# A DiT block kernel: two gates' modulation computed in later FFNs, and no background dot beside a slice's last column tile

## The chip, the cores and the metric

The kernel runs on one core of one Trainium2 chip. A core has five engines that matter here: TensorE (PE in the profile; its weight loads are listed apart as PEld), VectorE (DVE), ScalarE (ACT), GpSimd (POOL) and SyncE (SP), whose queue issues nearly all DMA transfers. Each engine works through its own instructions in order; they wait for each other through semaphores. The metric is the device time of one execution in microseconds.

## The reference

Two layers of a diffusion transformer with width 1024, on 512 latent and 256 context tokens. Each layer is an FFN, a token mixer (a gated DeltaNet group beside a multi-head latent attention group), and a second FFN:

```python
m = silu(c) @ w_ada[l] + b_ada[l]            # 9 vectors of 1024 for the latent tokens, and 9 for the context
def pre_mod(x, g, m, slot):
    return rmsnorm(x, g) * (1 + m[3 * slot + 1]) + m[3 * slot]
def post_residual(x, y, g, m, slot, weight):
    return x + weight * m[3 * slot + 2] * rmsnorm(y, g)
def ffn_sublayer(x, m, slot, ...):            # d_ff = 2816
    h = pre_mod(x, g_pre, m, slot)
    y = (silu(h @ wg) * (h @ wu)) @ wd
    return post_residual(x, y, g_post, m, slot, 0.5)
for l in range(2):
    x = ffn_sublayer(x, m, 0, ...)            # first FFN
    x = post_residual(x, mixer(pre_mod(x, g, m, 1)), g, m, 1, 1.0)
    x = ffn_sublayer(x, m, 2, ...)            # second FFN; in layer 1 for the latent tokens alone
```

The nine vectors of a layer are numbered (slot, part): slot 0 is the first FFN, 1 the mixer, 2 the second FFN; part 0 is the shift, 1 the scale, 2 the gate that `post_residual` multiplies with. The modulation of a gate is therefore needed only when its sublayer's output is there.

## The kernel before

Everything is fp32. A weight or an activation is split into a rounded part `whi` or `gh` (type fp32r) and the rest `wlo` or `gl`, and each product is made of three matmuls: high by high, high by low, low by high. A weight tile comes by DMA into one of four buffers (`wraw`, 128x1024, 512 KB), ScalarE copies it to `whi` (L93) and GpSimd or VectorE subtracts to get `wlo` (L94).

**An FFN** (`ffn`, L522) takes the 22 column tiles of 128 of its hidden width in six slices of 4, 4, 4, 4, 2, 4 tiles. The first three tiles of slice 0 are computed as written in the reference. From the fourth on a tile is a *split tile* (`fast`, L586): gate and up products are formed from seven half products, 384 of the 768 tokens each (256 in the last FFN), with sums of weights and of activations formed on VectorE. The names in it: `prod` issues the 12 matmuls of a half product (L606 to L608); `u2`, `u4`, `c12`, `p1` are sums on VectorE; `out` (L611) forms the gated result at its end: an add (L614), a multiplication (L615), ScalarE's copy to `gh` (L616) and VectorE's subtraction to `gl` (L617). After a slice, `down` (L755) multiplies its tiles with the down weights and adds into y (eight row tiles, in pairs; L773, L774 and L776 are the matmuls with `gh`, `gl`, and `wlo`). Within the first pair the slice's last tile comes last.

**Background dots.** Of the modulation `m`, what is not needed at once is computed on VectorE beside the FFNs. `ada_bg(l, slot, parts, vecs)` (L351) puts one job for each of eight weight rows of each part on a list, and a closing one that adds the bias and forms the gate or scale; a job's DMA brings a row block of 512 KB (`abraw`, in the same four buffers as `wraw`), and its one or two dots (L241, 128x1024 with `srow`; one for the latent vector, one for the context vector; in the trace their output is named `adot` or `abraw`) reduce it to a column of `raw`. A *dot* below is one such L241 instruction of 128x1024; the short L241 rows of 128x1 read the sum out.

**What sets the order.** `pump` (L114) is called 58 times in an FFN: twice for tile 2, twice in each split tile, once for each row chunk in `down`, but never in the last slice's `down`. Each call adds `rate` to a credit, the number of jobs at the FFN's start divided by 57, and takes jobs from the list while the credit is at least 1. The credit is never set back: what is left goes on to the next FFN. Jobs that are left at the last slice's end are run by `flush` ahead of the residual (`p0` and `p2` in `body`, L1925 and L1957). The Tile framework's scheduler then orders each engine's instructions with a simulated timeline, within what the data and buffers allow; `high_priority` around the adds of a tile pulls these ahead of other work. So a dot stands not exactly where `pump` put it.

`body` (L1903) runs, for l = 0 and 1: `ada_bg` for the mixer and the second FFN, the first FFN, the mixer, for l = 0 `ada_bg` for layer 1's first FFN, and the second FFN. That gives 112, 48, 64 and 0 dots in the four FFNs.

Of the kernel before, what the change touches and what calls it, by code (L numbers as in the profile page):

```python
# [34 lines left out]
class K:  # L35
# [61 lines left out]
    def hp(self, on):  # L97
        return self.tc.high_priority(offset=on if on > 1 else None) if on else contextlib.nullcontext()
# [12 lines left out]
            self.ahead = nxt()  # L111
        fn(w)

    def pump(self):  # L114
        self.credit += self.rate
        if self.ahead is None and self.bg and self.bg[0][0]:
            self.ahead = self.bg[0][0]()
            return
        ran = False
        while self.credit >= 1 and self.bg:  # L120
            if self.bg[0][0] is None and ran:
                break
            ran = True
            self.credit -= 1
            self.bg_next()
# [396 lines left out]
    def ffn(self, l, i, slot, groups, post, begin=None):  # L522
# [7 lines left out]
        def loads(f, eng=None):  # L530
            return [self.load_w(d["wu"][l, i, f, u], eng=eng) for u in range(2)]
# [7 lines left out]
        def evac(j, pg, pu, off, n):  # L539
            for o in range(0, n, 256):  # L540
                sg = self.sg()[:, :256]
                c = slice(o, o + 256)
                with self.tc.high_priority():
                    nc.scalar.activation(sg, pg[:, c], AF.Silu)
                    nc.vector.tensor_tensor(out=sg, in0=pu[:, c], in1=sg, op=ALU.mult)  # L545
                gated(j, sg, off + o, 256)
# [32 lines left out]
        def combine_t1(F):  # L579

            for k in range(4):
                h, lo = F["t1"][k]
                nc.scalar.copy(h, self.y[k][:, :nh])
                nc.vector.tensor_sub(lo, self.y[k][:, :nh], h.bitcast(F32))

        def fast(f, j, F):  # L586


            lo_, hi_ = slice(0, 512), slice(512, 1024)
            wg, wu = self.raw(d["wu"][l, i, f, 0]), self.raw(d["wu"][l, i, f, 1])  # L590
            V = nc.vector
            w0 = self.cut(wg)
            w2 = self.cut(wu[:, hi_], 512, V)
            V.tensor_sub(wg[:, lo_], wg[:, lo_], wu[:, lo_])
            V.tensor_add(wu[:, lo_], wu[:, lo_], wu[:, hi_])
            V.tensor_sub(wu[:, hi_], wu[:, hi_], wg[:, lo_])
            V.tensor_sub(wg[:, hi_], wg[:, hi_], wu[:, hi_])
            w3 = self.cut(wu, eng=V)
            w1 = self.cut(wg, eng=V)

            def prod(w, half, xs):
                ps = self.bank()[:, :nh]
                for k in range(4):
                    c = slice(half * 512 + k * P, half * 512 + (k + 1) * P)
                    xh, xl = F[xs][k]
                    nc.tensor.matmul(ps, w[0][:, c], xh, start=k == 0, stop=False)  # L606
                    nc.tensor.matmul(ps, w[0][:, c], xl, start=False, stop=False)  # L607
                    nc.tensor.matmul(ps, w[1][:, c], xh, start=False, stop=k == 3)  # L608
                return ps

            def out(ps, u, sl, off):  # L611

                gx, gy = gh[j][:, off : off + nh], gl[j][:, off : off + nh]
                V.tensor_add(ps, u, ps)  # L614
                V.tensor_mul(ps, ps, sl)  # L615
                nc.scalar.copy(gx, ps)  # L616
                V.tensor_sub(gy, ps, gx.bitcast(F32))  # L617

            T = lambda n: self.sg(n)[:, :nh]
            hp = self.tc.high_priority  # L620
            ps = prod(w0, 0, "b11")
            p1 = T("p1")
            with hp():
                nc.scalar.copy(p1, ps)
            ps = prod(w3, 1, "t2")
            u2 = T("u2")
            with hp():
                V.tensor_add(u2, p1, ps)
            ps = prod(w0, 1, "b21")
            with hp():  # L630
                V.tensor_add(p1, p1, ps)
                nc.scalar.activation(p1, p1, AF.Silu)
            ps = prod(w3, 0, "t1")
            u4 = T("u4")
            with hp():
                V.tensor_add(u4, u2, ps)
            self.pump()
            ps = prod(w1, 1, "b22")
            c12 = T("c12")
            with hp():  # L640
                V.tensor_add(c12, u4, ps)
                nc.scalar.activation(c12, c12, AF.Silu)
            ps = prod(w1, 0, "t3")
            with hp():
                V.tensor_add(u2, u2, ps)
                out(ps, u4, c12, nh)
            ps = prod(w2, 0, "t4")
            with hp():
                out(ps, u2, p1, 0)
            self.pump()  # L650

        if begin is not None:
            next(begin)
        for s, nf in enumerate(SLICES):
            gh = [self.fp.tile([P, NT], F32R, tag=f"gh{j}", name=f"gh{j}") for j in range(nf)]
            gl = [self.fp.tile([P, NT], F32R, tag=f"gl{j}", name=f"gl{j}") for j in range(nf)]
            f0 = SL0[s]
# [68 lines left out]
            if s == 0:  # L726
                self.drain()
                F = combine()
            for j in range(j0, nf):
                if f0 + j > 2:  # L730
                    if f0 + j == 3:
                        combine_t1(F)
                    fast(f0 + j, j, F)
                    continue
                ps = []
                pre = s == 0 and j == 2 and W2
                W = [None, self.load_w(d["wu"][l, i, 2, 1])] if pre else loads(f0 + j)
                for u in range(2):
                    if pre and u == 0:
                        ps.append([(pl, 0, NL)] + ([(pc[:, :256], NL, NC)] if has_c else []))  # L740
                        self.pump()
                        continue
                    wh, wl = W[u]
                    outs = [(self.bank()[:, :n], off, n) for off, n in full]
                    for k in range(KT):
                        self.mm3(outs, wh[:, k * P : (k + 1) * P], wl[:, k * P : (k + 1) * P], k, k == 0, k == KT - 1)
                    ps.append(outs)
                    if u == 0:
                        self.pump()
                for (pg, off, n), (pu, _, _) in zip(*ps):  # L750
                    evac(j, pg, pu, off, n)
                self.pump()
# [1150 lines left out]
def body(tc, dram, out, stop=None):  # L1903
    k = K(tc, dram, out)
    nc = k.nc
    k.psp = k.pool("psum", space=PSUM)
    k.drp = k.pool("dram", space=DRAM)
    k.ph = 'start'
    k.consts()
    k.open_w()  # L1910
    k.open_z()
    k.open_f()
    k.ada_bg(0, 0, [2], [0, 1])
    for l in range(2):
        last = l == 1
        if l == 0:
            k.ada_bg(0, 1, [0, 1, 2], [0, 1])
            k.ada_bg(0, 2, [0, 1, 2], [0, 1])
        else:
            k.ada_bg(1, 1, [0, 1], [0, 1])  # L1920
            k.ada_bg(1, 1, [2], [0])
            k.ada_bg(1, 2, [0, 1, 2], [0])
        k.rate = len(k.bg) / 57

        def p0(g, ss):  # L1925
            k.flush()
            return k.post(l, 0, g, ss, nxt=(l, 1))

        k.ph = f'F1_{l}'
        k.ffn(l, 0, 0, GROUPS, p0, k.begin() if l == 0 else None)  # L1930
        k.mix_pre(l)
        k.drain()
        xd = k.dram_tile(f"xd{l}", [KT, P, NT])
        for kt in range(KT):
            nc.sync.dma_start(xd[kt], k.X[kt])
        k.close(k.fp)
        k.ph = f'M1_{l}'
        k.mix_in(l, last)
        k.close_z()
        k.close(k.wp)  # L1940
        k.ph = f'G_{l}'
        k.gdn(l, last)
        k.open_zs(range(6))
        k.gdn_out(l, last)
        k.ph = f'A_{l}'
        k.mla(l, last)
        if stop == f"o_{l}":
            for j in range(8):
                nc.gpsimd.dma_start(out[:, j, 0], k.zh[j].bitcast(F32))
                nc.gpsimd.dma_start(out[:, j, 1], k.zl[j].bitcast(F32))  # L1950
            return finish(k, False)
        k.open_f()

        def p1(g, ss):
            return k.post(l, 1, g, ss, nxt=(l, 2))

        def p2(g, ss):  # L1957
            k.flush()
            return k.post(l, 2, g, ss, final=last, nxt=(l + 1, 0))

        k.ph = f'O_{l}'
        k.mix_out(l, last, xd, p1)
        if not last:
            k.ada_bg(1, 0, [0, 1, 2], [0, 1])
        k.rate = len(k.bg) / 57
        k.ph = f'F2_{l}'
        k.ffn(l, 1, 2, GROUPS[1:] if last else GROUPS, p2)
        if last or stop:
            k.drain()
        if stop == f"f2_{l}":  # L1970
            return dump_x(k)
    finish(k)


def dump_x(k):
    for kt in range(KT):
        k.nc.sync.dma_start(k.out[:, kt], k.X[kt])
    finish(k)
# [31 lines left out]
```

## Time and profile before

| | |
|---|---|
| runs of the kernel | 3344.32, 3345.82, 3350.79 us (median 3345.82) |
| the profiled execution | 3344.23 us |
| its span in the trace | 3342.5 us |
| granted clock of TensorE, mean of the span | 0.951 |
| TensorE busy, matmuls | 3078.1 us (92%) |
| TensorE busy, weight loads | 2805.2 us (84%) |
| VectorE busy | 2545.8 us (76%) |
| ScalarE busy | 1376.5 us (41%) |
| GpSimd busy | 1359.4 us (41%) |

Busy time counts how long an engine had an instruction in work; matmuls are pipelined and their ends are modelled. The granted clock is a share of full speed, 2.4 GHz. TensorE is busy for 92% of the span, so what can be gained lies in its waits and in the stretches in which it runs at less than full clock. The share is a mean over stages with different limits, and the mixers' waits are in it as well.

### The profile page before, as it was taken

The page shows a single profiled execution, that of the slowest core. Times are in us where ns is not written, and L with a number is a line of the kernel's source. Part 1 is how long each engine was busy: PE and PEld are TensorE (multiplying, and loading weights), DVE is VectorE, ACT ScalarE, POOL GpSimd, SP SyncE. Part 2 cuts the span into 40 slices and gives each one's busy share as a digit, 9 for nine tenths or more (in the row PEclk, how much of TensorE's full clock was granted, in tenths as well). Part 3 has the DMA queues.
Part 4 walks back from the last instruction along what each step waited for, and adds up shares of the span by engine and source line. Part 5 has one row for each costly group of instructions (what it writes and reads, how often), then busy time and mean ns, then how long its engine had stood idle before and what let it go on. Part 6 is the DMA issues. An engine that isn't in the chain of part 4 may idle for free. (4 is left out here: it accounts for less than half of the span.)

```text
span 3342.5 us, 53690 instructions
## 1 busy us (share of the span) xinstructions
PE 3078.1 (92%) x20836; PEld 2805.2 (84%) x20836; DVE 2545.8 (76%) x4336; ACT 1376.5 (41%) x2600; POOL 1359.4 (41%) x1060
## 2 busy tenths in 40 slices
PE   7899999889898999999999799999988788899998
PEld 4799888877786788899999799999977676789998
DVE  7888888777779858677777977677687879876676
ACT  4332223454345645333324432323454445554343
POOL 5321221543556665322214522221554556753233
PEclk8999999989998999999999899999989899899999
DMA  6233343321310032223324233342322310223233
GB/s 232 89 127 119 114 144 103 120 68 50 111 47 27 21 107 83 89 95 107 101 70 145 68 122 120 120 145 89 108 91 58 102 46 5 88 77 114 89 108 95
DMA packets 149815, 318.68 MB, mean 95 GB/s; under 512 B 38184, under 2 KB 79528, under 8 KB 149560
## 3 DMA queue, kind: packets, MB, share of 16 engines
q1 hardware_dynamic: 149560, 315.25, 29.0%
q8 instruction: 163, 2.67, 0.3%
q14 instruction: 92, 0.75, 0.1%
HBM read 285.17 MB, written 30.03 MB: 94 GB/s over the span
## 5 line engine op out<-in xcount | busy, mean ns | idle before, releaser
L94 POOL TENSOR_TENSOR wlo<-wraw,whi 128x1024 fp32r<-128x1024 f32 (+1 forms) x228 | 589.5, 2595 | 1356.5 <-ACT whi L93 1261.1
L93 ACT CAST whi<-wraw 128x1024 fp32r<-128x1024 f32 (+2 forms) x482 | 469.0, 977 | 700.4 <-PE ps L774 341.6
L517 PE MATMUL ps<-zh,whi 128*128 128x256 f32 (+1 forms) x1208 | 394.1, 336 | 24.6 <-DVE sg L545 13.3
L606 PE MATMUL ps<-zh,whi 128*128 128x384 f32 (+1 forms) x1216 | 391.3, 322 | 3.5 <-DVE sg L545 2.9
L607 PE MATMUL ps<-zl,whi 128*128 128x384 f32 (+1 forms) x1216 | 390.8, 321 | 0.0
L608 PE MATMUL ps<-zh,wlo 128*128 128x384 f32 (+1 forms) x1216 | 390.3, 321 | 0.0
L518 PE MATMUL ps<-zl,whi 128*128 128x256 f32 (+1 forms) x1208 | 381.4, 327 | 4.1 <-DVE zl L475 4.1
L773 PE MATMUL ps<-gh,whi 128*128 128x512 f32 (+1 forms) x1008 | 349.4, 354 | 29.9 <-ACT gh L616 27.2
L520 PE MATMUL ps<-zh,wlo 128*128 128x256 f32 (+1 forms) x1208 | 352.5, 326 | 0.0
L774 PE MATMUL ps<-gl,whi 128*128 128x512 f32 (+1 forms) x1008 | 339.7, 352 | 12.1 <-DVE gl L617 12.1
L94 DVE TENSOR_TENSOR wlo<-wraw,whi 128x1024 fp32r<-128x1024 f32 (+1 forms) x254 | 289.2, 1139 | 41.2 <-ACT whi L93 39.7
L776 PE MATMUL ps<-gh,wlo 128*128 128x512 f32 (+1 forms) x1008 | 297.0, 351 | 0.0
L517 PEld LDWEIGHTS ps<-zh,whi 128*128 128x128 f32 x1208 | 240.0, 203 | 57.3 <-DVE sg L545 14.6
L518 PEld LDWEIGHTS ps<-zl,whi 128*128 128x128 f32 x1208 | 240.1, 199 | 23.7 <-DVE zl L475 5.1
L773 PEld LDWEIGHTS ps<-gh,whi 128*128 128x128 f32 x1008 | 192.3, 193 | 74.5 <-ACT gh L616 30.2
L606 PEld LDWEIGHTS ps<-zh,whi 128*128 128x128 f32 x1216 | 229.2, 189 | 5.6 <-DVE sg L545 1.9
L241 DVE CUSTOM_DVE_ANT_0 abraw<-abraw,srow 128x1024 f32<-128x1024 f32 x128 | 202.6, 1582 | 38.7 <-DMA abraw<-in_wat 36.4
L607 PEld LDWEIGHTS ps<-zl,whi 128*128 128x128 f32 x1216 | 229.2, 188 | 0.4
L608 PEld LDWEIGHTS ps<-zh,wlo 128*128 128x128 f32 x1216 | 229.0, 188 | 0.0
L774 PEld LDWEIGHTS ps<-gl,whi 128*128 128x128 f32 x1008 | 193.4, 192 | 42.0 <-DVE gl L617 16.5
L520 PEld LDWEIGHTS ps<-zh,wlo 128*128 128x128 f32 x1208 | 223.4, 199 | 6.1 <-POOL zl L475 0.6
L606 PE MATMUL ps<-t42h,whi 128*128 128x384 f32 (+1 forms) x608 | 197.8, 325 | 2.8 <-ACT whi L93 2.8
(394 smaller groups left out, 7686.4 us busy)
## 6 DMA issues: line engine op xcount, KB each, us to landing
wraw<-in_wu SPq DMA_DIRECT2D x176, 512.0 KB, 3.4
abraw<-in_wat SPq DMA_DIRECT2D x128, 512.0 KB, 4.1
wraw<-in_wd SPq DMA_DIRECT2D x88, 512.0 KB, 3.4
wraw<-in_wi SPq DMA_DIRECT2D x44, 512.0 KB, 3.3
wraw<-in_wo SPq DMA_DIRECT2D x16, 512.0 KB, 3.9
xs<-x SPq DMA_DIRECT2D x64, 128.0 KB, 1.7
x<-xs SPq DMA_DIRECT2D x64, 128.0 KB, 3.4
x<-in_x SPq DMA_DIRECT2D x48, 128.0 KB, 3.6
```

Of the source, the lines that this page charges most:

```text
L93: nc.scalar.copy(hi[:, :n], raw[:, :n])
L94: (eng or nc.gpsimd).tensor_sub(lo[:, :n], raw[:, :n], hi[:, :n].bitcast(F32))
L241: self.nc.vector.tensor_tensor_reduce(out=dst, in0=w, in1=self.srow[:, v, a:b], scale=1.0, scalar=start, op0=ALU.mult, op1=ALU.add, accum_ ...
L517: nc.tensor.matmul(ps, wh, self.zh[k][:, off : off + n], start=first, stop=False)
L518: nc.tensor.matmul(ps, wh, self.zl[k][:, off : off + n], start=False, stop=False)
L520: nc.tensor.matmul(ps, wl, self.zh[k][:, off : off + n], start=False, stop=last)
L606: nc.tensor.matmul(ps, w[0][:, c], xh, start=k == 0, stop=False)
L607: nc.tensor.matmul(ps, w[0][:, c], xl, start=False, stop=False)
L608: nc.tensor.matmul(ps, w[1][:, c], xh, start=False, stop=k == 3)
L773: nc.tensor.matmul(ps, wh[:, o : o + P], gh[j][:, off : off + n], start=j == 0, stop=False)
L774: nc.tensor.matmul(ps, wh[:, o : o + P], gl[j][:, off : off + n], start=False, stop=False)
L776: nc.tensor.matmul(ps, wl[:, o : o + P], gh[j][:, off : off + n], start=False, stop=j == nf - 1)
```

## The change

Two edits are made. First, `pump` takes an argument; a split tile that is the last of its slice calls it with a false value, and then it adds to the credit and starts no job, so that the jobs come at the next call, which is one in `down`. Second, the gates are put on the list later: the gate of layer 0's second FFN on the list of that FFN, layer 1's first gate on the list of the FFN that it belongs to, and layer 1's last gate on the list of the last FFN. The four FFNs get 96, 48, 72 and 8 dots. Lines from L116 on stand two further down than before.

```diff
-    def pump(self):
+    def pump(self, now=True):
         self.credit += self.rate
+        if not now:
+            return
...
-        def fast(f, j, F):
+        def fast(f, j, F, bg):
...
-            self.pump()
+            self.pump(bg)
             ps = prod(w1, 1, "b22")
...
-            self.pump()
+            self.pump(bg)
...
-                    fast(f0 + j, j, F)
+                    fast(f0 + j, j, F, j < nf - 1)
...
         if l == 0:
             k.ada_bg(0, 1, [0, 1, 2], [0, 1])
-            k.ada_bg(0, 2, [0, 1, 2], [0, 1])
+            k.ada_bg(0, 2, [0, 1], [0, 1])
         else:
+            k.ada_bg(1, 0, [2], [0, 1])
             k.ada_bg(1, 1, [0, 1], [0, 1])
             k.ada_bg(1, 1, [2], [0])
-            k.ada_bg(1, 2, [0, 1, 2], [0])
+            k.ada_bg(1, 2, [0, 1], [0])
...
-        if not last:
-            k.ada_bg(1, 0, [0, 1, 2], [0, 1])
+        if last:
+            k.ada_bg(1, 2, [2], [0])
+        else:
+            k.ada_bg(0, 2, [2], [0, 1])
+            k.ada_bg(1, 0, [0, 1], [0, 1])
```

VectorE, first FFN of layer 0, the last tile of slice 1, from the add to `c12` to the last `gl`, before (the rows left out read a dot's sum):

```order
L641 TENSOR_TENSOR c_1926<-u_1906,ps 128x384
L241 ISA adot,raw_1_0_140<-abraw,srow 128x1024
...
L645 TENSOR_TENSOR u_1876<-u_1876,ps 128x384
L614 TENSOR_TENSOR ps<-u_1906,ps 128x384
L241 ISA abraw,raw_1_0_140<-abraw,srow 128x1024
...
L614 TENSOR_TENSOR ps<-u_1876,ps 128x384
L241 ISA adot,raw_1_0_140<-abraw,srow 128x1024
...
L615 TENSOR_TENSOR ps<-ps,c_1926 128x384
L615 TENSOR_TENSOR ps<-ps,p_1861 128x384
L241 ISA abraw,raw_1_0_140<-abraw,srow 128x1024
...
L617 TENSOR_TENSOR gl_1390<-ps,gh_1386 128x384 x2
```

The same place in the changed kernel:

```order
L643 TENSOR_TENSOR c_1911<-u_1896,ps 128x384
L243 ISA adot,raw_1_0_140<-abraw,srow 128x1024
...
L223 TENSOR_TENSOR m_1_0_3511<-raw_1_0_140,cols 128x16
L647 TENSOR_TENSOR u_1866<-u_1866,ps 128x384
L616 TENSOR_TENSOR ps<-u_1896,ps 128x384
L243 ISA abraw,raw_1_0_140<-abraw,srow 128x1024
...
L616 TENSOR_TENSOR ps<-u_1866,ps 128x384
L617 TENSOR_TENSOR ps<-ps,c_1911 128x384
L617 TENSOR_TENSOR ps<-ps,p_1851 128x384
L619 TENSOR_TENSOR gl_1385<-ps,gh_1381 128x384 x2
L243 ISA adot,raw_1_0_140<-abraw,srow 128x1024
```

Between the add to `c12` and the last `gl` there were four dots and now are two; the dot between the last multiplication and `gl` has gone, and one that stood between the two adds of L614 (now L616) and the multiplications now follows `gl`.

VectorE in layer 1, the end of the output projection and the start of the last FFN: squares' sums (`be`, L403), copies to y (L1789) and the row factors' scaling (`rba`, L156), before:

```order
L403 TENSOR_TENSOR be<-be,bt 128x256
L432 SCALAR_TENSOR_TENSOR x_27757<-bt,m_1_2_20072,x_27757 128x256
L1789 COPY y_27718<-ps 128x256
L403 TENSOR_TENSOR be<-be,bt 128x256
L1789 COPY y_27719<-ps 128x256
L403 TENSOR_TENSOR be<-be,bt 128x256
L1789 COPY y_27720<-ps 128x256
L156 TENSOR_SCALAR rba<-rb 128x2
L403 TENSOR_TENSOR be<-be,bt 128x256
L156 TENSOR_SCALAR rba<-rb 128x2
```

The same place in the changed kernel:

```order
L243 ISA abraw,raw_2_2_28310<-abraw,srow 128x1024
...
L405 TENSOR_TENSOR be<-be,bt 128x256
L434 SCALAR_TENSOR_TENSOR x_27732<-bt,m_1_2_20600,x_27732 128x256
L1791 COPY y_27693<-ps 128x256
L405 TENSOR_TENSOR be<-be,bt 128x256
L243 ISA abraw,raw_2_2_28310<-abraw,srow 128x1024
...
L1791 COPY y_27694<-ps 128x256
L243 ISA abraw,raw_2_2_28310<-abraw,srow 128x1024
...
L405 TENSOR_TENSOR be<-be,bt 128x256
L1791 COPY y_27695<-ps 128x256
L243 ISA abraw,raw_2_2_28310<-abraw,srow 128x1024
...
L158 TENSOR_SCALAR rba<-rb 128x2
```

Four dots of the last FFN's list now stand among these rows, where none stood.

VectorE in layer 0's second FFN, from the weight sums of its first split tile (L595 to L597) to its first add (L628), before:

```order
L595 TENSOR_TENSOR wraw<-wraw 128x512
L545 TENSOR_TENSOR sg<-ps,sg 128x256 x3
L596 TENSOR_TENSOR wraw<-wraw 128x512
L537 TENSOR_TENSOR gl_12439<-sg,gh_12435 128x256 x3
L597 TENSOR_TENSOR wraw<-wraw 128x512
L94 TENSOR_TENSOR wlo<-wraw,whi 128x1024 x2
L628 TENSOR_TENSOR u_13148<-p_13133,ps 128x384
```

The same place in the changed kernel:

```order
L597 TENSOR_TENSOR wraw<-wraw 128x512
L547 TENSOR_TENSOR sg<-ps,sg 128x256 x3
L598 TENSOR_TENSOR wraw<-wraw 128x512
L243 ISA adot,raw_2_2_12389<-abraw,srow 128x1024
...
L539 TENSOR_TENSOR gl_12397<-sg,gh_12393 128x256 x3
L599 TENSOR_TENSOR wraw<-wraw 128x512
L243 ISA abraw,raw_2_2_12389<-abraw,srow 128x1024
...
L94 TENSOR_TENSOR wlo<-wraw,whi 128x1024 x2
L630 TENSOR_TENSOR u_13111<-p_13096,ps 128x384
```

Two dots now stand between the weight sums and the `wlo` subtractions of the summed weights. TensorE in layer 1's first FFN, in its first split tile behind the product with `b11` (`t42h` and `t42l`, `zh` and `zl`, `t` are the operands of the half products; four of the seven take the summed weights, whose `wlo` is cut last), before:

```order
L606 MATMUL ps<-t42h,whi 128x384
L607 MATMUL ps<-t42l,whi 128x384
L606 MATMUL ps<-zh_9567,whi 128x384
L607 MATMUL ps<-zl_9568,whi 128x384
L608 MATMUL ps<-zh_9567,wlo 128x384
L606 MATMUL ps<-zh_9569,whi 128x384
L607 MATMUL ps<-zl_9570,whi 128x384
L608 MATMUL ps<-t42h,wlo 128x384
```

The same place in the changed kernel, where the product with `zh_9567` is complete already:

```order
L608 MATMUL ps<-t42h,whi 128x384
L609 MATMUL ps<-t42l,whi 128x384
L608 MATMUL ps<-zh_9522,whi 128x384
L609 MATMUL ps<-zl_9523,whi 128x384
L608 MATMUL ps<-zh_9524,whi 128x384
L609 MATMUL ps<-zl_9525,whi 128x384
L608 MATMUL ps<-t_18077,whi 128x384
L609 MATMUL ps<-t_18077,whi 128x384
L608 MATMUL ps<-t42h,whi 128x384
L609 MATMUL ps<-t42l,whi 128x384
L610 MATMUL ps<-t42h,wlo 128x384
...
L610 MATMUL ps<-t42h,wlo 128x384 x2
```

Before, the `wlo` of a summed weight was wanted by the 20th matmul of the tile; now four products are begun without their `wlo`, one that takes no summed weight is run to its end, and the 45th matmul is the first that wants such a `wlo`. In layer 0's second FFN it is the 45th before and now.

## Rows read from the trace of the kernel before

**Rows 1.** Windows of three FFNs' bodies: stretch, us, busy (count) by engine, clock, DMA, GB/s.

```profile
178.00:592.00 414.00, 393.16 (x2185) 373.73 (x2184) 350.50 (x563) 124.03 (x177) 93.03 (x35) 0.97 0.36 121
1400.00:1788.00 388.00, 383.81 (x2189) 367.69 (x2188) 281.05 (x451) 124.72 (x178) 91.70 (x35) 1.00 0.29 93
3042.00:3301.00 259.00, 259.00 (x1852) 243.92 (x1851) 187.38 (x345) 112.14 (x176) 87.91 (x35) 1.00 0.32 98
```

**Rows 2.** Waits of TensorE, whole trace: line, releaser, us in total, times, longest.

```profile
PE ps L773 <- ACT gh L616: 27.2, 10, 5.3
...
PE ps L774 <- DVE gl L617: 12.1, 10, 2.1
```

**Rows 3.** Windows of down stretches: slices 1 to 3, first FFN; slice 1, second.

```profile
236.60:277.80 41.20, 35.94 (x195) 30.72 (x194) 35.20 (x57) 6.29 (x9) 5.22 (x3) 0.92 0.38 129
336.50:379.70 43.20, 36.42 (x194) 30.84 (x193) 34.64 (x55) 6.38 (x10) 7.91 (x3) 0.92 0.37 124
438.40:478.40 40.00, 36.71 (x194) 31.18 (x193) 32.94 (x53) 6.28 (x9) 7.07 (x3) 0.91 0.41 133
1458.50:1492.20 33.70, 33.70 (x194) 29.45 (x193) 20.98 (x33) 4.56 (x7) 4.88 (x2) 1.00 0.25 82
```

**Rows 4.** Timeline of TensorE, those slices: start, duration, instruction, wait and its releaser.

```profile
248.40 1.68 PE L773 MATMUL ps<-gh,whi 128*128 128x256 f32 x4 [5.26 <-ACT gh L616]
...
346.64 0.50 PE L773 MATMUL ps<-gh,whi 128*128 128x256 f32 x2 [3.65 <-ACT gh L616]
350.27 1.22 PE L773 MATMUL ps<-gh,whi 128*128 128x512 f32 x2 [3.13 <-ACT gh L616]
...
447.10 1.69 PE L773 MATMUL ps<-gh,whi 128*128 128x256 f32 x4 [2.20 <-ACT gh L616]
449.88 0.58 PE L774 MATMUL ps<-gl,whi 128*128 128x256 f32 x1 [1.09 <-DVE gl L617]
```

**Rows 5.** Timeline of VectorE, first FFN, end of slice 1.

```profile
240.65 3.05 DVE L241 CUSTOM_DVE_ANT_0 abraw<-abraw,srow 128x1024 f32<-128x1024 f32 x1
...
243.63 0.55 DVE L614 TENSOR_TENSOR ps<-u,ps 128x384 f32<-128x384 f32 x1
244.10 3.25 DVE L241 CUSTOM_DVE_ANT_0 adot<-abraw,srow 128x1024 bf16<-128x1024 f32 x1
...
248.22 1.21 DVE L241 CUSTOM_DVE_ANT_0 abraw<-abraw,srow 128x1024 f32<-128x1024 f32 x1
...
249.36 1.01 DVE L617 TENSOR_TENSOR gl<-ps,gh 128x384 fp32r<-128x384 f32 x2
```

**Rows 6.** Timeline of GpSimd, the same place.

```profile
240.22 2.40 POOL L94 TENSOR_TENSOR wlo<-wraw,whi 128x1024 fp32r<-128x1024 f32 x1 [3.14 <-ACT whi L93]
```

**Rows 7.** All dots: count, ns (shortest, median, longest), first to last start.

```profile
L241 DVE CUSTOM_DVE_ANT_0 abraw<-abraw,srow x128: 1206/1219/3203, 65.4 to 2292.8; 128x1024 f32<-128x1024 f32 x128
L241 DVE CUSTOM_DVE_ANT_0 adot<-abraw,srow x96: 1206/1224/3479, 62.2 to 2003.1; 128x1024 bf16<-128x1024 f32 x96
```

**Rows 8.** Timeline of TensorE, second FFN, ends of slices 0 and 3.

```profile
1373.53 0.50 PE L774 MATMUL ps<-gl,whi 128*128 128x512 f32 x1 [1.26 <-DVE gl L617]
...
1652.27 0.62 PE L774 MATMUL ps<-gl,whi 128*128 128x512 f32 x2 [1.85 <-DVE gl L617]
```

**Rows 9.** Timelines of VectorE and TensorE, start of the last FFN.

```profile
2958.14 0.43 DVE L403 TENSOR_TENSOR be<-be,bt 128x256 f32<-128x256 f32 x1 [0.71 <-ACT bt L402]
...
2961.01 0.42 DVE L403 TENSOR_TENSOR be<-be,bt 128x256 f32<-128x256 f32 x1 [2.02 <-POOL be L403]
...
2961.48 0.61 PE L153 MATMUL rb<-ones,be 128*128 128x1 f32 x4 [2.69 <-DVE be L403]
```

**Rows 10.** Timeline of TensorE, first split tiles, first and second FFN.

```profile
118.00 0.45 PE L606 MATMUL ps<-t42h,whi 128*128 128x384 f32 x1 [2.08 <-ACT whi L93]
...
1349.79 0.34 PE L606 MATMUL ps<-zh,whi 128*128 128x384 f32 x1
...
1351.88 0.33 PE L606 MATMUL ps<-zh,whi 128*128 128x384 f32 x1
```

## Prediction

> **What bounds the kernel now.** I read the busy shares of whole stretches first, then who waited for whom on TensorE, then the timelines at the places found. In the bodies of three of the four FFNs (from the second slice to the last tile) TensorE is busy for 393.2 of 414 us, 383.8 of 388 and 259 of 259 [rows 1]. So the first FFN of layer 0 loses about 21 us there, at a granted clock of 0.97, and the others next to nothing; VectorE is busy 350.5 of those 414 us, against 281.1 of 388 and 187.4 of 259. Among TensorE's waits for other engines in the whole trace stand those of the FFNs' down products: the first down matmul that reads the slice's last tile waits for `gh` (27.2 us, 10 times), and for `gl` there are 12.1 us (10 times) [rows 2]. Slices 1 to 3 of the first FFN have 5.26 us, 3.65 + 3.13 us and 2.20 + 1.09 us of it [rows 4].
>
> What such a place costs is read from the length of a whole down stretch. Stretches with the same work (194 matmul records, give or take one) take 41.2, 43.2 and 40.0 us in slices 1 to 3 of the first FFN, and 33.7 us in slice 1 of the second, where TensorE is busy throughout [rows 3]. The excess is 7.5 + 9.5 + 6.3 = 23.3 us. Waits are 15.3 of it; the other 8 us are matmuls after the wait at the lower of the clock's two levels (1.2 instead of 2.4 GHz): the granted clock of these stretches is 0.91 to 0.92, that of the undisturbed one 1.00.
>
> Why `gh` and `gl` are late is in [rows 5]. VectorE works there without a gap, and between the second add (243.63 us) and the last `gl` (249.36 us) it runs two background dots, of 3.25 and 1.21 us; just ahead of that add stands one of 3.05 us. The shortest dot of the trace takes 1.21 us, the longest 3.48 [rows 7], and the long ones lie against a `wlo` subtraction on GpSimd: that of 240.22 us ends at 242.62 us, and the dot begun at 240.65 us ends 1.08 us after it, at 243.70 us [rows 5, 6].
>
> **The change part by part.**
>
> *Slices 1 to 3 of the first FFN.* Eight of 56 weight rows (16 of 112 dots) leave this FFN, and none is started in a slice's last tile. The scheduler still drops older dots into that tile, so I count in VectorE's order the dots that stand in a slice ahead of its last `gl`: 16, 18 and 16 before, 14, 14 and 12 now. Two, four and four dots fewer, at 1.21 to 3.25 us each, are 2.4 to 6.5, 4.8 to 13 and 4.8 to 13 us of VectorE time, against waits of 5.26, 6.78 and 3.29 us. At the low price 2.9 + 2.0 + 0 us of waiting is left, and the clock falls at two of the places still (2.2 us each, the 8 us spread over three places, less a little for shorter waits): a gain of 23.3 - 4.9 - 4.4 = 14 us. At the high price all of the 23.3 us go. The dots at the end of a slice are mostly long ones ((3.05 + 3.25 + 1.21) / 3 = 2.5 us in [rows 5]), so I stay near the upper end and leave 1 us for each place, since the chain add, mul, copy to `gh`, `gl` starts only when the last product is there: **-20.3 us** (-14 to -23.3).
>
> The Trainium skill ("SBUF — State Buffer", Who interferes with whom) says that a VectorE instruction with two SBUF inputs and a GpSimd instruction that reads SBUF exclude each other, and that whichever issues first holds the port to its end. Read against this change, it warns that a dot put beside the down products can hold up the weight cuts that GpSimd makes there. In the down stretch of slice 1 GpSimd works only 5.2 of 41.2 us [rows 3], so by this trace there is little to hold up, and the sum stays; if each of three dots held a cut for 1.21 us in each of the three places, they would give back up to 11 us.
>
> *Slices 0 and 4 of the first FFN.* The order at their ends is the same as before, dot for dot: 0 (-3 to +3, if a transfer for a dot lands sooner or later).
>
> *The dots that wait for the down stretch* now run in a bunch ahead of the first adds into y: three, 3.6 us, where one or two stood. TensorE fills other PSUM banks meanwhile, and no wait for a bank shows in [rows 2 to 4]. 0 (up to +2 in each of three places).
>
> *The second FFN of layer 0* keeps 48 dots. In slice 0 the dot between the last `mul` and the last `gl` goes, and slice 3 gets the order that slice 1 has now, whose stretch is the undisturbed one of [rows 3]; their waits are 1.26 and 1.85 us [rows 8]: -3.1 us.
>
> *The starts of the FFNs.* Credit that skipped calls leave is carried on. In the first FFN the order has four dots fewer ahead of the last cuts of its first split tile, where TensorE waits 2.08 us for such a cut [rows 10]: -1 us. In the second FFN two more stand there, in the third two more (and two fewer ahead of its last row factors), and its slice 1 has four more (14 for 10). Unhidden, two dots cost 2.4 to 6.8 us. But TensorE's order has 44 matmuls of the split tile ahead of the first that wants a late `wlo`, in the second before and now, in the third now (19 before); twelve take 2.1 us [rows 10], so this is some 7.7 us of cover. I take +1 for the second (0 to +5) and +1.5 for the third, slice 1 included (-2 to +8).
>
> *The last FFN* gets eight dots where it had none. Four stand among the row sums and row factors ahead of its first products. VectorE idles 0.71 and 2.02 us there, and TensorE waits 2.69 us for the sum [rows 9]: 4 x 1.21 = 4.8 us, less 2.7 us of idling, is 2.1 us; with a GpSimd instruction in the way of one it is 4 us or more. A fifth stands ahead of the first cuts, 1.2 us. Three are hidden (VectorE is idle for 72 of 259 us, [rows 1]). **+3.5** (0 to +8).
>
> Sum: -20.3 - 1 - 3.1 + 1 + 1.5 + 3.5 = -18.4 us. The profiled execution took 3344.2 us (its span 3342.5), so 3325.8 us; the median of the runs lies 1.6 us above it. I say 3327 us.
>
> **The rivals.**
>
> *Slower: the carried credit decides.* Thirteen dots more (2 + 2 + 4 + 5) stand where TensorE is about to start on fresh weights, row factors or a last tile. For it: such places are short of VectorE time, and a dot beside a cut on GpSimd takes up to 3.48 us. Against it: TensorE's order gives 7.7 us of cover at two of the starts, and the starts wait for GpSimd and ScalarE too. At 3 us each they cost 39 us against 24.4 us gained elsewhere, so +14.6: 3360 us. It decides from 24.4 / 13 = 1.9 us a dot.
>
> *The change does not do what it says.* Five dots still stand in the last tile of slices 1 to 3. If `gl` comes as late as now in slices 1 and 2, because it is the dots left that meet GpSimd, only slice 3 and the second FFN gain: -6.3 - 3.1 + 6 = -3.4, with the median's 1.6 us 3342 us. For it: the long dots are long through GpSimd, not through their number. Against: VectorE has no gap there, so whatever is taken out ahead moves `gl` forward.
>
> *More than forecast.* A VectorE with 16 dots less in the first FFN catches up in slices 0 and 4 too, and the starts hide what they get. The waits of [rows 2] are 39.3 us, and by the three places above the clock adds 8 / 15.3 of that, 20 us: 60 us are there to be had, and half of them with nothing lost elsewhere make -30 to -35: 3312 us. Against: the order at those ends has not changed.
>
> **How the numbers follow.** Forecast 0.62 (its own range 3318 to 3336), slower rival 0.06, no effect 0.18, more 0.14. What a measurement of this kernel can tell from no change is about 0.2%, 6.7 us: faster is below 3339, slower above 3352.5. Faster: 0.62 + 0.14 + a quarter of 0.18 = 0.80; slower 0.05, since a part of that rival ends within the bound; same 0.15. Cutting into the two outer cases for 2 in 10 gives 3311 to 3343 us.
>
> **What would show it.** The down stretches of slices 1 to 3 in the first FFN should take 34 to 36 us at a clock near 1.00, and the waits for `gh` and `gl` fall from 39.3 us to below 25. Slices 0 and 4 should look as before. The last FFN's row factors should come 2 to 5 us later behind the last products of the output projection. The forecast is wrong if those down stretches stay above 39 us, or if the starts lose over 20 us.

## The result and the profile after

The changed kernel takes 3325.07 us (median of 6 runs, 3320.87 to 3331.93), the kernel before 3347.57 us in the same comparison; the ratio is 0.9937, with a 95% interval of 0.9926 to 0.9948. Forecast were 3327 us. The sum came out; two of its terms missed by 10 us and more, and stages for which nothing was forecast made up for most of it.

The first lines of the page after, the span and the busy times:

```profile
span 3320.0 us, 53695 instructions
...
PE 3058.4 (92%) x20836; PEld 2785.7 (84%) x20836; DVE 2562.9 (77%) x4337; ACT 1377.4 (41%) x2600; POOL 1345.7 (41%) x1060
```

The windows of down stretches after, columns as in [rows 1]: slices 1 to 3 of the first FFN, which answer to [rows 3], then slices 1 and 2 of the third FFN (34.6 and 35.2 us long before), then slice 1 of the second.

```profile
230.70:269.30 38.60, 35.44 (x195) 30.77 (x195) 32.21 (x55) 7.00 (x10) 6.84 (x3) 0.96 0.42 145
327.40:366.90 39.50, 35.85 (x196) 30.79 (x195) 33.09 (x57) 6.66 (x9) 5.44 (x3) 0.96 0.45 154
424.90:461.00 36.10, 34.56 (x196) 29.61 (x195) 26.51 (x46) 6.42 (x9) 6.07 (x2) 1.00 0.36 126
1995.10:2035.70 40.60, 36.88 (x195) 31.64 (x194) 33.11 (x57) 6.59 (x9) 5.83 (x3) 0.92 0.44 150
2093.80:2132.70 38.90, 35.35 (x195) 30.67 (x195) 24.43 (x41) 6.41 (x9) 5.54 (x3) 0.96 0.33 112
1432.10:1465.80 33.70, 33.70 (x195) 29.51 (x195) 18.79 (x34) 6.42 (x9) 4.77 (x2) 1.00 0.27 94
```

The first FFN's three stretches lost 2.6, 3.7 and 3.9 us by these windows, and none but the third came near the undisturbed 33.7. The third FFN's slice 1 now looks as the first FFN's slices did: 40.6 us at a clock of 0.92. TensorE's waits in the whole trace (releaser: us, times, longest), for [rows 2]:

```profile
PE ps L775 <- ACT gh L618: 18.9, 8, 4.0
PE ps L776 <- DVE gl L619: 17.3, 8, 3.5
```

They are 36.2 us where 39.3 stood: what left the first FFN came back in the third. TensorE's timeline at the first FFN's slices 1 to 3, for [rows 4]:

```profile
240.30 1.69 PE L775 MATMUL ps<-gh,whi 128*128 128x256 f32 x4 [3.17 <-ACT gh L618]
...
334.76 0.50 PE L775 MATMUL ps<-gh,whi 128*128 128x256 f32 x2 [0.91 <-ACT gh L618]
...
338.00 0.39 PE L776 MATMUL ps<-gl,whi 128*128 128x256 f32 x1 [2.74 <-DVE gl L619]
...
433.36 0.39 PE L776 MATMUL ps<-gl,whi 128*128 128x256 f32 x1 [1.42 <-DVE gl L619]
```

8.2 us of waiting is left of 15.3. VectorE and then GpSimd at the end of slice 1, for [rows 5, 6]:

```profile
235.82 2.97 DVE L243 CUSTOM_DVE_ANT_0 abraw<-abraw,srow 128x1024 f32<-128x1024 f32 x1
...
240.28 1.02 DVE L619 TENSOR_TENSOR gl<-ps,gh 128x384 fp32r<-128x384 f32 x2
```

```profile
235.31 2.38 POOL L94 TENSOR_TENSOR wlo<-wraw,whi 128x1024 fp32r<-128x1024 f32 x1 [3.13 <-ACT whi L93]
```

Between the first of the adds on L616 (L614 before) and the last `gl` stands one dot where three stood, but it is a long one: it ends 1.1 us after GpSimd's cut, as in [rows 5, 6].

To compare whole stages I took from TensorE's timeline the time from each FFN's first split tile to its first down, the length of every down stretch, the stretches between two downs, and what lies between the FFNs; of each kernel from two profiles, of which the second is in the experiments below (spans 3342.5 and 3343.4 before, 3320.0 and 3329.6 after). Means in us:

| stage | before | after | difference | forecast |
|---|---|---|---|---|
| first FFN, up to its first down | 134.6 | 132.2 | -2.4 | -1 |
| first FFN, downs of slices 1 to 3 | 124.5 | 114.3 | -10.2 | -20.3 |
| first FFN, downs of slices 0 and 4 | 70.4 | 68.1 | -2.3 | 0 |
| second FFN, start | 14.9 | 16.2 | +1.3 | +1 |
| second FFN, downs | 160.4 | 155.2 | -5.2 | -3.1 |
| third FFN, start and downs | 184.1 | 196.5 | +12.4 | +1.5 |
| last FFN, first split tile to first down | 19.6 | 20.6 | +1.1 | +3.5 with what lies ahead |
| stretches between downs, last FFN's downs | 857.0 | 849.8 | -7.3 | 0 |
| between the FFNs: mixers, last slices | 1767.7 | 1762.3 | -5.4 | 0 |
| sum | 3333.2 | 3315.1 | -18.1 | -18.4 |

### The profile page after: what moved, and what is told of

Its sections match the earlier page's. It is cut to its first block, busy times and chain, and to the rows that moved or that the text cites. A ratio compares the mean times of both kernels' runs of the same rounds, so it can differ in the third digit from the quotient of the medians.

```text
span 3320.0 us, 53695 instructions
## 1 busy us (share of the span) xinstructions
PE 3058.4 (92%) x20836; PEld 2785.7 (84%) x20836; DVE 2562.9 (77%) x4337; ACT 1377.4 (41%) x2600; POOL 1345.7 (41%) x1060
## 5 line engine op out<-in xcount | busy, mean ns | idle before, releaser
L94 POOL TENSOR_TENSOR wlo<-wraw,whi 128x1024 fp32r<-128x1024 f32 (+1 forms) x228 | 580.3, 2554 | 1357.5 <-ACT whi L93 1304.9
L94 DVE TENSOR_TENSOR wlo<-wraw,whi 128x1024 fp32r<-128x1024 f32 (+1 forms) x254 | 298.1, 1175 | 31.3 <-ACT whi L93 29.9
L776 PEld LDWEIGHTS ps<-gl,whi 128*128 128x128 f32 x1008 | 193.5, 192 | 46.7 <-DVE gl L619 19.6
L243 DVE CUSTOM_DVE_ANT_0 adot<-abraw,srow 128x1024 bf16<-128x1024 f32 x96 | 151.3, 1576 | 63.2 <-DMA abraw<-in_wat 62.8
```

Source lines behind the costliest of these rows:

```text
L94: (eng or nc.gpsimd).tensor_sub(lo[:, :n], raw[:, :n], hi[:, :n].bitcast(F32))
L243: self.nc.vector.tensor_tensor_reduce(out=dst, in0=w, in1=self.srow[:, v, a:b], scale=1.0, scalar=start, op0=ALU.mult, op1=ALU.add, accum_ ...
L776: nc.tensor.matmul(ps, wh[:, o : o + P], gl[j][:, off : off + n], start=False, stop=False)
```

## Experiments

The theory I began with: the dots that stand ahead of a slice's last `gl` set the waits, and the change pays by taking some away. Each kernel's ratio is to the kernel before, in runs on the same chip.

**pump_only, moves_only: which of the two edits pays?**

pump_only is the changed kernel with the three gates on their old lists, of which one shows here:

```diff
-            k.ada_bg(0, 2, [0, 1], [0, 1])
+            k.ada_bg(0, 2, [0, 1, 2], [0, 1])
```

moves_only is the changed kernel with jobs started in every split tile:

```diff
-                    fast(f0 + j, j, F, j < nf - 1)
+                    fast(f0 + j, j, F, True)
```

> Only the first edit: split tiles that end a slice start no job; the gates stay on their old lists (112, 48, 64, 0 dots). In VectorE's order the dots ahead of the last gl of the first FFN's slices 1 to 3 are 16, 18, 16 as before, and 7, 9, 7 of them stand in the last tile (6, 7, 6 before). Theory (what counts is how many dots the scheduler puts ahead of gl, and the gates' move is what lowers it): no gain, 0 to +8 us, ratio 1.000 to 1.0025. Rival (starting no job in the last tile is what pays): about the whole gain, -15 to -22 us, ratio 0.9935 to 0.9955.

> Only the second edit: the gates on the later lists (96, 48, 72, 8 dots), jobs started in every split tile as before. In the order 14, 14, 12 dots stand ahead of the last gl of the first FFN's slices 1 to 3, 4 of them in the last tile (5 in the changed kernel). Theory: the whole gain of the change or a little more, -18 to -26 us, ratio 0.992 to 0.9945. Rival (the first edit pays): no gain, ratio 0.999 to 1.001.

Measured: pump_only 3354.97 us, 1.0014 (1.0005 to 1.0023); moves_only 3325.51 us, 0.9925 (0.9913 to 0.9938). The move of the gates pays all of it, and the argument of `pump` costs a little: moves_only is 5 us faster than the changed kernel on the same chip (3330.64 us in again_after, below). The move also brings the longer list of calls, whose effect on addresses is taken up with pad576. pump_only's down windows of the first FFN's slices 1 to 3:

```profile
233.70:276.60 42.90, 37.37 (x195) 31.98 (x194) 35.96 (x58) 6.98 (x10) 6.22 (x3) 0.88 0.39 132
335.10:379.70 44.60, 37.02 (x196) 31.42 (x194) 37.38 (x58) 6.97 (x10) 8.98 (x4) 0.92 0.42 136
438.20:481.40 43.20, 37.52 (x196) 32.12 (x195) 32.47 (x50) 7.04 (x10) 6.36 (x3) 0.88 0.36 119
```

They are longer than before by 1.7, 1.4 and 3.2 us ([rows 3]). Behind the add to `c12` in the last tiles of these slices its trace has 4, 5 and 4 dots, as many as before; the changed kernel has 2, 2 and 2. A program that starts no job in a tile has not said that no dot shall stand there: the scheduler puts it where its own timeline has room. The credit that is kept also shows. From the first split tile to the first down the second and third FFNs take 14.6 and 14.7 us in moves_only, 16.2 and 16.6 in the changed kernel, 15.8 and 16.7 in pump_only.

**gate_back, again_after: is the third FFN's loss that of its dots?**

```diff
-            k.ada_bg(1, 0, [2], [0, 1])
...
-            k.ada_bg(1, 0, [0, 1], [0, 1])
+            k.ada_bg(1, 0, [0, 1, 2], [0, 1])
```

> The changed kernel with layer 1's first gate put back on the list of layer 0's second FFN (96, 64, 56, 8 dots). Theory (the third FFN's down stretches, 12 us longer than before, pay for its 8 more dots and its 14 dots in slice 1): they come back to the lengths of before, -8 to -12 us there; the second FFN gets 10 dots in each of slices 1 to 3 where it had 6 to 10, +1 to +5: net -3 to -10 us against the changed kernel, ratio 0.991 to 0.993 to the kernel before. Rival (the third FFN lost by chance or by the carried credit alone): not better than the changed kernel, 0.9935 to 0.995.

> The changed kernel itself, as the measure for the three others on the same chip, and a second profile of it. Theory and rival alike: ratio 0.993 to 0.995. If the 58.5 us stretches between two downs, which lie wholly on TensorE, take 58.1 us again, the 0.4 us that they gained belong to the kernel; at 58.5 us they belong to the execution that was profiled.

Measured: gate_back 3335.08 us, 0.9957 (0.9944 to 0.9969); again_after 3330.64 us, 0.9944 (0.9932 to 0.9957). The mechanism holds and the size does not. The third FFN's downs fall from 180 to 168 us, as expected, but the second FFN's rise from 155 to 168.5, not by 1 to 5. Eight weight rows cost 12 to 13 us in the downs of either FFN. again_after has the 58.1 us stretches again, so these belong to the kernel.

**pad576, again_before: the 0.4 us of each stretch.**

The stretches of four split tiles between two downs take 58.5 us in the kernel before and 58.1 in the changed one, mostly without a wait. pad576 is the kernel before with one dummy tile:

```diff
         self.srow = cp.tile([P, 2, 1024], F32, name="srow")
+        pad = cp.tile([P, 144], F32, name="pad")
+        nc.gpsimd.memset(pad, 0.0)
```

> The kernel before with one dummy tile of 576 bytes a partition among the constants, which is what the three more tiles for dot columns take in the changed kernel: y, the operands t42 and t, gh and gl move to the addresses that they have there; the orders at the FFNs' slices stay. Theory A (the 0.4 us that each of the 58.5 us stretches between two downs gained comes from these addresses: the matmuls on t42 and t fell from 176 to 173 ns, those on zh and zl stayed): the stretches take 58.1 us, some 5 us less in all FFNs and a few more in the mixers, ratio 0.9965 to 0.9985. Theory B (it comes from what VectorE does at the time): 58.5 us as before, ratio 0.9995 to 1.0005.

> The kernel before, profiled a second time: by theory A of pad576 its stretches between two downs take 58.5 us again; and it shows how far the lengths of the other stretches vary from one profile to the next (estimate: 1 us in an FFN's stretch, 3 us in a mixer).

Measured: pad576 3338.3 us, 0.9972 (0.996 to 0.9984); theory A holds. Its stretches take 58.1 us, those of again_before 58.5. The view of the first product's line in one such stretch of the second FFN (count: shortest, median, longest ns, first and last start), of the kernel before:

```profile
L606 PE MATMUL ps<-zh,whi x64: 332/334/346, 1492.2 to 1546.2; 128*128 128x384 f32 x64
L606 PE MATMUL ps<-t42h,whi x32: 336/337/343, 1494.3 to 1550.4; 128*128 128x384 f32 x32
```

and of the changed kernel:

```profile
L608 PE MATMUL ps<-zh,whi x64: 334/334/338, 1465.6 to 1519.2; 128*128 128x384 f32 x64
L608 PE MATMUL ps<-t42h,whi x32: 331/335/339, 1467.7 to 1523.4; 128*128 128x384 f32 x32
```

From the first to the last matmul on `t42h` it is 56.1 us in the one and 55.7 in the other, with the same order of work and no wait. again_before also gives the scatter: in the third FFN slice 2 takes 35.2 us in one profile of the same kernel and 39.0 in the other, and a stretch of the first FFN 3.6 us more, with a wait for a `wlo`.

**nodots: what all the dots cost.**

```diff
-                self.ada_dot(raw[:, pi, k, v : v + 1], w, v, 0, 1024, keep=v != vecs[-1])
+                self.nc.vector.tensor_copy(raw[:, pi, k, v : v + 1], w[:, 0:1])
```

> The changed kernel with each background dot replaced by a copy of one column (its products are left out; the transfers stay). Theory (dots are what makes gh and gl late): all down stretches of the first three FFNs take 33.7 to 34 us, TensorE's waits for gh and gl fall from 36 us to below 6: ratio 0.981 to 0.986. Rival (the long chain of add, multiplication, copy and subtraction and the cuts on GpSimd make them late, the dots only fill in): waits stay above 20 us, ratio above 0.989.

Measured: 3247.54 us, 0.9694 (0.9681 to 0.9708), more than expected. All downs of four tiles take 33.7 us, and one row is left of TensorE's waits for the last tile:

```profile
PE ps L776 <- DVE gl L619: 1.9, 3, 0.9
```

So the dots make `gh` and `gl` late, not the chain itself. The end of the second FFN and the start of the third, where `flush` runs, are 11 us shorter as well.

**cut_dve: why a dot takes up to 3.4 us.**

```diff
-            return self.load_w(wd[:, base + c * 1024 : base + (c + 1) * 1024])
+            return self.load_w(wd[:, base + c * 1024 : base + (c + 1) * 1024], eng=None if last else nc.vector)
```

> The changed kernel with the wlo cuts of the down weights on VectorE instead of GpSimd (all but the last slice). Theory (a dot takes 2 to 3.4 us instead of 1.2 because GpSimd cuts a weight at the same time: 58 of the 69 long dots of the changed kernel overlap a cut there, 22 of 155 short ones do): the number of dots above 1.3 us falls from 69 to below 30; VectorE has four cuts of 1.2 us more in each down, 19 downs or 91 us in all, against some 80 us of dots that get short, so the time stays within 10 us of the changed kernel: ratio 0.991 to 0.997. Rival (dots are long for another reason, such as their transfers): as many long dots as now, and the time 10 us or more above it.

Measured: 3329.34 us, 0.9941 (0.9924 to 0.9959); 33 of 224 dots take over 1.3 us where it was 69, and all dots together 308 us instead of 359. So GpSimd's cuts are what made most of the others long. Fewer than expected went because GpSimd keeps other work: 21 of the 33 begin under a cut of weights that stayed with it, and the other 12 overlap another GpSimd instruction, as each of the 69 does in the changed kernel. The time stays, since VectorE now does the cuts itself: it is busy for 2574.5 us where it was 2562.9.

**pinned, pin_before, pin_moves, pin_pad: keep the dots out by a dependency.**

The first two lines stand in `ada_dot`, the others in `down` after each row chunk:

```diff
+        if self.pin is not None:
+            self.nc.vector.tensor_copy(out, self.pin.bitcast(F32))
...
+                    self.pin = gl[nf - 1][:, 0:1]
                     self.pump()
+                    self.pin = None
```

> The changed kernel, but each dot of a job that is started in a slice's down stretch first writes its result column from the last gl (80 ns), so that the scheduler can't put it ahead of that gl. In the order 0 to 3 dots are left ahead of a slice's last gl (12 to 14 in the first FFN before). Theory (dots ahead of gl are what delays the first pair): the excess of the down stretches goes, about 13 us in the first FFN's slices 1 to 3, 8 in its slice 0 and 22 in the third FFN: ratio 0.983 to 0.988 to the kernel before. Rival (they can't all go into the downs: the first FFN has 19 dots, 23 us, for each down, where VectorE has 12.7 us idle in an undisturbed one, so the adds into y and the next tile's weight sums come late): the first FFN gives back 10 us a slice, ratio 0.992 to 0.998.

> The kernel before (both edits undone) with the pin of the run pinned alone: dots started in a down stretch write their column from the last gl first. No dot is left in a slice's last tile of the first FFN in the order, 6 or 7 in the slices. Theory (where the dots stand decides, neither the lists nor the calls): most of the gain of pinned without the changed kernel's edits; its excess over undisturbed downs is 42 us in the first FFN, 8 in the second and 13 in the third, and some 10 us may come back as 112 dots crowd the first FFN: ratio 0.982 to 0.986. Rival (112 dots don't fit into the first FFN's downs, the move of the gate is needed): 0.988 to 0.993.

> The run pinned without the first edit (jobs are started in every split tile again). Theory (the first edit does nothing for where the dots end up): 0.979 to 0.982, as pinned. Rival (with the pin the first edit counts, since it leaves more dots to the down): 0.984 or more.

> pin_before with the dummy tile of pad576: the old lists and calls, the pin, and the changed kernel's addresses. Theory (with the pin the changed kernel's two edits are worth their addresses alone): pin_before's 0.9793 times pad576's 0.9972 is 0.9766, so 0.9755 to 0.9780, level with pin_moves (0.977). Rival (the shorter list of the first FFN still counts with the pin): 0.979 or more.

Measured: pinned (on the changed kernel) 3281.46 us, 0.98 (0.9787 to 0.9813); pin_before (on the kernel before) 3279.92 us, 0.9793 (0.9775 to 0.9811); pin_moves 3272.17 us, 0.977 (0.9755 to 0.9785); pin_pad 3265.39 us, 0.9743 (0.973 to 0.9756), the fastest kernel here. All are faster than expected. pin_pad's windows of the downs of slices 1 and 2 in the first FFN and slice 1 in the third:

```profile
219.80:253.50 33.70, 33.70 (x195) 29.49 (x194) 32.22 (x62) 6.01 (x9) 7.39 (x3) 1.00 0.44 144
311.60:345.30 33.70, 33.70 (x196) 29.49 (x195) 31.98 (x61) 5.54 (x7) 7.43 (x3) 1.00 0.46 143
...
1963.70:1997.40 33.70, 33.70 (x195) 29.50 (x195) 27.27 (x48) 5.85 (x8) 4.79 (x2) 1.00 0.49 163
```

TensorE has no idle time and full clock there, while VectorE is busy for 32.2 of 33.7 us. The same dots, 112 of them in the first FFN, cost these downs nothing behind the last `gl`; ahead of it they cost up to 10 us a slice. They are not free everywhere: in the first FFN slice 4's downs and the last slice's products take 83 us together in pin_pad, 82 in pad576 and 76 in nodots. In pinned the first two downs still take 38.0 and 39.4 us; TensorE waits there for down weights, up to 2.2 us at a time, and not for `gh` or `gl`. The copy takes 145 ns, not 80, and stands before 106 of pinned's 224 dots. The pin keeps more dots out than those that are pinned: in the order dots that were started in earlier tiles stand behind `gl` too. Why these follow was not tried. With it neither edit of the change is needed: pin_pad, with the old lists and calls, is no slower than pin_moves.

## Why the prediction was right, and where it was not

**What bounds the kernel** held: dots ahead of `gl`, the wait of the first pair, and the clock after it. nodots and pin_pad take all three away and get the undisturbed 33.7 us of [rows 3] in all downs of four tiles in the first three FFNs.

**Slices 1 to 3 of the first FFN: -20.3 forecast, -10.2 measured.** This term was mis-sized. The step that failed is the price of the dots that go: I took the mean of those in [rows 5], 2.5 us, and stayed near the upper end; my own lower end, -14, was still too far. In the traces the dots that stand in these slices ahead of the last `gl` took 81 us before and 69 after. Ten dots fewer gave back 11.8 us, 1.2 each, since 17 of 50 were over 1.3 us before and 15 of 40 still are. Counted from the start of its down stretch, the last `gl` ends 3.1, 4.2 and 2.9 us sooner, and 8.2 us of waiting are left where my low price had left 4.9. A dot has two prices, 1.2 us and up to 3.4, by whether GpSimd cuts a weight beside it, and which dots meet a cut is not told by how many stand there. The third FFN's slice 1 shows it. There the changed kernel and moves_only have the same sequence in the last tile. VectorE's timeline of the changed kernel:

```profile
1999.38 2.11 DVE L243 CUSTOM_DVE_ANT_0 adot<-abraw,srow 128x1024 bf16<-128x1024 f32 x1
...
2002.35 2.42 DVE L243 CUSTOM_DVE_ANT_0 abraw<-abraw,srow 128x1024 f32<-128x1024 f32 x1
...
2005.18 1.19 DVE L619 TENSOR_TENSOR gl<-ps,gh 128x384 fp32r<-128x384 f32 x2
```

and of moves_only:

```profile
2006.52 2.13 DVE L243 CUSTOM_DVE_ANT_0 adot<-abraw,srow 128x1024 bf16<-128x1024 f32 x1
...
2009.52 1.22 DVE L243 CUSTOM_DVE_ANT_0 abraw<-abraw,srow 128x1024 f32<-128x1024 f32 x1
...
2011.13 1.19 DVE L619 TENSOR_TENSOR gl<-ps,gh 128x384 fp32r<-128x384 f32 x2
```

GpSimd's rows there, of the changed kernel and then of moves_only:

```profile
1997.98 2.43 POOL L94 TENSOR_TENSOR wlo<-wraw,whi 128x1024 fp32r<-128x1024 f32 x1 [2.62 <-ACT whi L93]
2000.56 3.14 POOL L94 TENSOR_TENSOR wlo<-wraw,whi 128x1024 fp32r<-128x1024 f32 x1 [0.15 <-ACT whi L93]
```

```profile
2005.16 2.41 POOL L94 TENSOR_TENSOR wlo<-wraw,whi 128x1024 fp32r<-128x1024 f32 x1 [2.66 <-ACT whi L93]
2010.39 2.58 POOL L94 TENSOR_TENSOR wlo<-wraw,whi 128x1024 fp32r<-128x1024 f32 x1 [2.81 <-ACT whi L93]
```

In both the first dot begins under the first cut and takes 2.1 us. In the one the second cut covers the second dot's start, in the other it begins when the dot is nearly done. TensorE waits 0.98 + 2.73 us in the first and 0.77 + 0.48 in the second, and the down takes 40.6 against 35.8 us. The Trainium skill ("SBUF — State Buffer", Who interferes with whom) says that a VectorE instruction with two SBUF inputs and a GpSimd instruction that reads SBUF exclude each other, and that the first to issue keeps the port to its end. The traces agree: the 58 dots over 1.3 us that begin under a cut in the changed kernel all end 1.1 us behind it. I had read the rule for dots that hold up cuts; it was the cuts that held up the dots.

**The third FFN: +1.5 forecast, +12.4 measured.** The step that failed took its slice 1 as nearly hidden. The start cost +1.7 us, as the cover of 44 matmuls allowed; the downs cost 10.7, half of it in slice 1, where 14 dots stand for 10. The other half came in slices 2 and 3 (+2.2 and +3.2), which no term named; slice 3 has 8 dots in both kernels, but the one ahead of its last `gl` now takes 3.1 us where it took 1.8. The +12.4 lie outside the +8 of that term. I had priced dots in the first FFN at 2.5 us and in the third at next to nothing, with the same sequence.

**The addresses** were in no step. The longer list of `ada_bg` calls makes three more tiles of dot columns, 576 bytes, and everything allocated behind them moves. pad576 has 0.28% from that alone, some 9 us of the change's 21; the stretches without a wait make 5.5 of them. So by the ratios the dots' new order is worth about 12 us (5 either way, from the two intervals), where I forecast 18. This takes the two parts to add up, which is not shown: with the pin the same dummy tile is worth 17 us (0.9793 to 0.9743, 7 either way). Of the 5.4 us between the FFNs I can't say how much is from there: the same stages scatter by 5.6 us between two profiles of the kernel before.

**The smaller terms.** The second FFN's slice ends (-3.1, measured -5.2) and start (+1, +1.3) were right in sign and near in size. In the last FFN TensorE's wait for the sum of squares grew from 2.69 us [rows 9] to 4.86 in the changed kernel, a new wait of 1.86 us stands ahead of it, and the start takes 1.1 us more: some 5 us by these rows, against +3.5.

```profile
2939.73 0.59 PE L155 MATMUL rb<-ones,be 128*128 128x1 f32 x2 [4.86 <-DVE be L405]
```

**The rivals.** "No effect" had the right reason for what the three places fell short, that the dots left meet GpSimd, but `gl` did come sooner in each. "The carried credit decides" had its places right, but they cost 4 us at the three later starts and 5 in the third FFN's slice 1, not 39. What I gave as signs did not come: the downs were to take 34 to 36 us and the waits to fall below 25; above 39 us, the sign of being wrong, is slice 2 alone. By these the term of slices 1 to 3 was known to be wrong while the time was right.

**The total** came out by luck. Slices 1 to 3 and the third FFN were 21 us worse than forecast together, and the other rows of the table 20.6 better; 12.7 of these lie in the two rows for which the prediction had no term, the stretches between downs and what is between the FFNs.

## What to carry to other kernels

Not starting work at a place in the program is not the same as keeping it away from there, when a scheduler orders the engines: read the order, and use a dependency where the place matters. Price a filler instruction by whom it meets, not by its median, and put it behind the last result that the bottleneck engine waits for: there the same dots left the downs undisturbed. When a time comes out as forecast, compare the stages all the same, since 21 us too much one way and 21 the other stood in this one.

## What was not expected of the hardware

A matmul's time hangs on addresses in SBUF: on `t42` and `t` it was 176 ns from start to start in the timeline at the kernel before's addresses and 173 in pad576, at the same clock; on `zh` and `zl`, with the same weight tiles, 174 in both. That it is the address of the moving operand (`t42`, `t`, `zh`, `zl`) is inferred from this difference; no run moves one operand alone. In gate_back (384 bytes) the last FFN's stretches of 39.9 us take 40.15 instead of 39.4, so another shift makes some matmuls slower. What about the address decides was not tried.
